# A decoder layer with RWKV-7 and forgetting attention: the order of the substitution's loads and copies, and the number format of two per-head sums

## The chip, the cores and the metric

The kernel runs on one core of a Trainium2 chip. The metric is device time in microseconds of one execution, here the median of three runs. Engines are called as in the profile: PE (TensorE, matmul), PEld (its weight loads), DVE (VectorE), ACT (ScalarE), POOL (GpSimd), SP (SyncE, which issues all the DMAs of this kernel).

## The reference

One layer over 1024 tokens of width 1024, in float32: a norm, one projection to 14 blocks of 128 columns for RWKV-7 and to those of a forgetting attention (8 heads of 64 for each of the two), the two groups of heads, an output projection, and a gated MLP with a causal convolution. What the change touches lies in the RWKV part:

```python
kk = heads(k * k_k)
kk = kk * lax.rsqrt(jnp.maximum(jnp.sum(kk * kk, axis=-1, keepdims=True), 1e-24))
k = k * (1.0 + (a - 1.0) * k_a)
y = wkv7_scan(r_h, w_h, k_h, v_h, -kk, kk * a_h)
...
bonus = jnp.sum(r_h * k_h * r_k, axis=-1, keepdims=True) * v_h
```

`wkv7_scan` is a recurrence over tokens, `S = S * w + (S a) b + v k`, one 64 x 64 state for each head.

## The kernel before, in words

**Stages.** First comes the RWKV stage: 8 units, a unit being two heads (a pair `p`, 128 channels on the partitions) and one half (`hf`) of the tokens, with the dense projections (`r_...` and `t_...` matmuls, groups 0 to 14) beside it. When all 8 units have their output, the attention starts (`s` scores, `t` transposes of the softmax, `po` value products, `tt` transposes of the output), with what is left of the dense work beside it; its last two head pairs ask for all dense groups. The output projection (`op`) may begin once the dense work is done. Then comes the MLP, which takes the rest of the span.

**A unit.** The recurrence is worked in chunks of 64 tokens. `front` loads keys and rates, sums squares over a head's channels (`ss`), and makes decayed operands. `gram` multiplies them to 64 x 64 matrices, whose masked triangles go to `ga` and `gr`. `taken_out` sends the 32 x 32 diagonal blocks of `ga` to DRAM (`dsub`). `inverse` brings them back as 128 partitions with a block's columns on each (`ml`, of 32 rows; `mw`, 8 of them, the block columns that a partition solves), and inverts the triangles by substitution: 30 steps of one multiplication and one addition on POOL, four memsets of the diagonal, and stores to DRAM (`dinv`). `placed` loads these as block-diagonal weights (`tbd`). `solve` starts with parts that don't need them (`z`), then multiplies by `tbd`, by the off-diagonal blocks and by `tbd` again (`x`, `l`, `xx`). `chain` runs the state through 8 chunks, and `output` norms and gates. `slots` turns keys and values and makes the second sum over a head's channels, `bps`, from `rk` = r k r_k. Both sums are a matmul with `oblk`, a 128 x 128 matrix with ones in its two 64 x 64 diagonal blocks: each column of the result is the sum over the column's head, on all its partitions.

**What sets the order.** Each step is a generator that yields instructions. A planner with a cost for each instruction picks at each moment the one that can start first on its engine, and among those that could start at once, the one with the lowest number in `RANK`; the dense work has 9, `inverse` 7, `placed` 6, `taken_out` 0. The result is one fixed order for each engine, and each engine works it off in that order, waiting where an operand is not there. Each of the nine steps of a unit is one stream (`each`) that takes the units one after the other. `ml`, `mw` and `ga` have one buffer each.

**Formats.** A float32 matmul runs as several passes. The dense projections instead split each operand into a part rounded to a shorter format (float32r, `hi`, a cast on ACT) and the rest (`lo`, a subtraction on DVE), and multiply those in one pass each. `Q.take(fp, ..., "f2", ..., 4)` takes one of four places of a ring in SBUF, when the place is free again; the evacuations of the dense matmuls draw from the same ring.

Of the kernel before, what the change touches and what calls it, by code (L numbers as in the profile page):

```python
# [8 lines left out]
F32 = mybir.dt.float32  # L9
F32R = mybir.dt.float32r  # L10
AF = mybir.ActivationFunctionType
ALU = mybir.AluOpType
# [4 lines left out]
P = 128  # L17
# [3 lines left out]
HALF = 512  # L21
# [11 lines left out]
INF = float("inf")  # L33

RANK = dict(rates=4, loads=2, params=4, fills=3, normed=4, turned=4, weights=3, splits=3, dense=9, evac=0, forget=8,
            chain=1, solve=2, inverse=7, taken_out=0, placed=6, front=3, gram=0, slots=4, output=5, stages=0, late_splits=8,
            late_loads=3, late=9, products=5, load_pairs=6, values=3, scores=0, soft=4, turned_back=2, tail=7,
            added=3, parts=1, summed=4, turned_again=4, combined=2, up_loads=6, sums=2.5, up_splits=2.5, down_loads=7,
            down_splits=2.5, token_loads=5, conv=9, combined_2=3,
# [235 lines left out]
def hymba_layer(tc, x, norm_mix_w, w_in, rwkv_mu, rwkv_w0, rwkv_w2, rwkv_a0, rwkv_a2, rwkv_g2, rwkv_k_k, rwkv_k_a,  # L275
# [3 lines left out]
    PE, V, S, G, SP = (Queue(k, e) for k, e in (("PE", nc.tensor), ("V", nc.vector), ("S", nc.scalar),  # L279
                                                ("G", nc.gpsimd), ("SP", nc.sync)))  # L280
    Q = Streams()

    whole = ExitStack()
    with whole:
        whole.enter_context(tc.manual_schedule())
        cst = whole.enter_context(tc.tile_pool(name="cst", bufs=1))
# [3 lines left out]
        ident = cst.tile([P, P], F32, name="ident")  # L290
        make_identity(nc, ident)
        Q.given.update([ident.name] + [f"in_{n}" for n in _INS])
        oblk = cst.tile([P, P], F32, name="oblk")
        ones = cst.tile([P, P], F32, name="ones")
        mhalf = cst.tile([P, 16], F32, name="mhalf")
        prm = cst.tile([P, C_END], F32, name="prm")
        cvw = cst.tile([P, 3, 2 * NFF], F32, name="cvw")
        Q.do(V.memset(mhalf, -0.5), V.memset(oblk, 0.0), V.memset(oblk[0:64, 0:64], 1.0),
             V.memset(oblk[64:128, 64:128], 1.0), V.memset(ones, 1.0),)


        sp_r = {(j, p, h): dr.tile([P, HALF], F32, name=f"sp_{j}_{p}_{h}") for j in "rkv" for p in range(4)
# [28 lines left out]
        fp = whole.enter_context(tc.tile_pool(name="fp", bufs=2))  # L331
# [8 lines left out]
        def bank(tag, name, bufs):  # L340
            t = yield from Q.take(pd if tag == "mm" else pr_, [P, HALF], F32, tag, name, bufs)
            return t
# [398 lines left out]
        def has(i, key):  # L741
            return lambda: i < 0 or key in units[i]

        def names(i):
# [11 lines left out]

            return p, hf, u, tl, rp, col

        def front(i):
            p, hf, u, tl, rp, col = names(i)  # L760
            q = units[i]
            yield lambda: ("rate", p, hf) in done and ("r", 4 + p, hf) in done
            xs = tl("t2", "xs", [P, HALF], 6)
            yield SP.dma_start(xs, sp_th[0, p, hf])
            kt_ = tl("ld", "k", [P, HALF], 2)
            yield SP.dma_start(kt_, sp_r["k", p, hf])
            ta = tl("t2", "ta", [P, HALF], 6)
            yield SP.dma_start(ta, sp_th[1, p, hf])
            k3 = kt_.rearrange("p (n c) -> p n c", c=C)


            sq = tl("t2", "sq", [P, HALF], 6)
            yield S.activation(sq, kt_, AF.Square, scale=col(C_KK))
            pt = yield from rp("ss")
            yield PE.matmul(pt, lhsT=oblk, rhs=sq, start=True, stop=True)
            beta = tl("t2", "beta", [P, HALF], 6)
            yield V.tensor_scalar(beta, pt, scalar1=1e-24, scalar2=0.0, op0=ALU.max, op1=ALU.add)
            Q.release(pt)

            cum = tl("cx", "cum", [P, 8, C + 1], 2)  # L780
            yield V.memset(cum[:, :, 0:1], 0.0)
            for n in range(8):
                yield V.tensor_tensor_scan(cum[:, n, 1:C + 1], xs[:, n * C:(n + 1) * C], ones[:, 0:C], 0.0,
                                           op0=ALU.add, op1=ALU.add)
            cr = tl("cx", "cr", [P, 8, C + 1], 2)
            yield V.tensor_tensor(cr, cum, cum[:, :, 32:33].to_broadcast([P, 8, C + 1]), op=ALU.subtract)
            ex = tl("cx", "ex", [P, 8, C + 1], 2)
            yield S.activation(ex, cr, AF.Exp, scale=-SDEC)


            em = tl("t2", "em", [P, HALF], 6)
            yield S.activation(em.rearrange("p (n c) -> p n c", c=C), cr[:, :, 1:C + 1], AF.Exp, scale=SDEC)
            ke = tl("t2", "ke", [P, HALF], 6)
            yield S.activation(ke, ta, AF.Identity, scale=hka[:, p:p + 1], bias=oka[:, p:p + 1])
            for n in range(4):
                yield V.reciprocal(beta[:, n * P:(n + 1) * P], beta[:, n * P:(n + 1) * P])
            yield lambda: ("r", p, hf) in done
            yield has(i - 1, "bonus")
            rt = tl("ld", "r", [P, HALF], 2)
            yield SP.dma_start(rt, sp_r["r", p, hf])  # L800
            r3 = rt.rearrange("p (n c) -> p n c", c=C)
            fx = Q.tile(sm, [P, 9], F32, "fx", f"{u}_fx", 2)
            yield V.tensor_tensor(fx[:, 0:7], cr[:, 0:7, C], cr[:, 1:8, 0], op=ALU.subtract)
            yield V.tensor_copy(fx[:, 7:8], cr[:, 7, C:C + 1])
            yield V.tensor_scalar(fx[:, 8:9], cr[:, 0, 0:1], scalar1=-1.0, scalar2=0.0, op0=ALU.mult, op1=ALU.add)
            yield has(i - 3, "chain")
            ff = Q.tile(sm, [P, 9], F32, "ff", f"{u}_ff", 3)
            yield S.activation(ff, fx, AF.Exp, scale=-SDEC)
            yield V.tensor_scalar(ta, ta, scalar1=0.5, scalar2=0.5, op0=ALU.mult, op1=ALU.add)
            yield V.scalar_tensor_tensor(ta, kt_, col(C_KK), ta, op0=ALU.mult, op1=ALU.mult)  # L810
            yield has(i - 1, "kbt")
            kb = tl("kb", "kb", [P, 4, 4, C], 1)
            ta4 = ta.rearrange("p (m o c) -> p m o c", o=2, c=C)
            em4 = em.rearrange("p (m o c) -> p m o c", o=2, c=C)
            ke4 = ke.rearrange("p (m o c) -> p m o c", o=2, c=C)
            yield V.tensor_tensor(kb[:, :, 0::3, :], ta4, em4, op=ALU.mult)
            yield V.tensor_tensor(ke, ke, kt_, op=ALU.mult)
            yield V.tensor_tensor(kb[:, :, 1:3, :], ke4, em4, op=ALU.mult)
            yield has(i - 1, "taken")
            ar = tl("ar", "ar", [P, 2, 8, C], 1)  # L820
            yield V.scalar_tensor_tensor(ar[:, 0], k3, nkk[:, p:p + 1], ex[:, :, 0:C], op0=ALU.mult, op1=ALU.mult)
            yield V.tensor_tensor(ar[:, 0], ar[:, 0], beta.rearrange("p (n c) -> p n c", c=C), op=ALU.mult)
            yield V.tensor_tensor(ar[:, 1], r3, ex[:, :, 1:C + 1], op=ALU.mult)
            yield V.scalar_tensor_tensor(rt, rt, col(C_RK), ke, op0=ALU.mult, op1=ALU.mult)
            q.update(kb=kb, ar=ar, ff=ff, rk=rt, front=True)
# [32 lines left out]
        def slots(i):  # L858

            p, hf, u, tl, rp, col = names(i)  # L860
            q = units[i]
# [24 lines left out]
            yield S.copy(vu4[0:64, :, 1, :], pt[64:128].rearrange("p (m c) -> p m c", c=P))  # L886
            Q.release(pt)
            q["vu"] = vu
            pt = yield from rp("bps")
            yield PE.matmul(pt, lhsT=oblk, rhs=q["rk"], start=True, stop=True)  # L890
            q["bonus"] = True
            yield V.tensor_tensor(bv, bv, pt, op=ALU.mult)
            Q.release(pt)
# [15 lines left out]
        def inverse(i):  # L909


            p, hf, u, tl, rp, col = names(i)
            q = units[i]
            yield has(i, "dsub")
            dsub = q["dsub"]
            dinv = dr.tile([8, 2, 2, 32, 32], F32, name=f"{u}_dinv")
            ml = tl("ml", "ml", [P, 32, 32], 1)
            mw = tl("mw", "mw", [P, 8, 32], 1)
            tmp = tl("mtmp", "mtmp", [P, 72], 1)
            mwf = mw.rearrange("p a t -> p (a t)")  # L920
            for g in range(4):
                gs = slice(g * 32, g * 32 + 32)
                yield SP.dma_start(ml[gs], dsub.rearrange("q o b s t -> (q o b) s t"))
                yield S.copy(mw[gs], ml[gs, g::4, :])
            for s in range(1, 31):
                w, n = 31 - s, (s + 3) // 4
                tv = tmp[:, 0:n * w].rearrange("p (s t) -> p s t", t=w)
                yield G.tensor_tensor(tv, mw[:, 0:n, s:s + 1].to_broadcast([P, n, w]),
                                      ml[:, s:s + 1, s + 1:32].to_broadcast([P, n, w]), op=ALU.mult)
                yield G.tensor_tensor(mw[:, 0:n, s + 1:32], mw[:, 0:n, s + 1:32], tv, op=ALU.add)  # L930
            for g in range(4):
                yield G.memset(mwf[g * 32:g * 32 + 32, g::36], 1.0)
            for g in range(4):
                yield SP.dma_start(dinv.rearrange("q o b s t -> (q o b) s t")[:, g::4, :],
                                   mw[g * 32:g * 32 + 32])
            q["dinv"] = dinv

        def placed(i):
            q = units[i]
# [1047 lines left out]
```

## Time and profile before

| | |
|---|---|
| three runs, us | 1462.61, 1462.68, 1465.28 |
| profiled execution, us | 1458.29 |
| its span, first to last instruction, us | 1456.5 |
| granted PE clock, mean | 0.996 |
| first score matmul of the attention, us from the span's start | 552.42 |

In slices of 1/40 of the span (36.4 us; digits are busy tenths) POOL shows where the substitution runs, and PE that it is full nearly everywhere but in the first slice, about the sixteenth to twentieth, and in the last:

```profile
PE   6999999999999999989999989999999999999997
POOL 3006553365465212433301000000000000000011
```

The costs on POOL: 240 multiplications (30 for each unit) and as many additions (columns: busy us and mean ns of one, then idle time before them and what ended it).

```profile
L193 POOL TENSOR_TENSOR u_mtmp<-u_mw,u_ml 128x60 f32<-128x60 f32 (+10 forms) x240 | 79.1, 330 | 147.7 <-ACT u_mw L193 129.6
L193 POOL TENSOR_TENSOR u_mw<-u_mw,u_mtmp 128x60 f32<-128x60 f32 (+10 forms) x240 | 83.9, 350 | 18.6
```

All instructions are recorded by one helper, so all have line 193; groups are told apart by their tiles. In the profile a unit's tiles are called `u_...`, whatever the unit.

### The profile page before, as it was taken

How to read it: one execution, taken by the hardware profiler on the slowest of the kernel's cores; microseconds unless marked ns; L12 is line 12 of the kernel's file. 1: busy time of each engine (PE TensorE's matmuls, PEld its weight loads, DVE VectorE, ACT ScalarE, POOL GpSimd, SP SyncE). 2: the span in 40 equal slices, each digit the busy share in tenths (PEclk: the TensorE clock that was granted, in tenths of full speed). 3: DMA queues.
4: the chain of work that ended last, by engine and by line, in shares of the span. 5: the costliest groups of instructions: out<-in, count | busy, mean ns of one | idle time of the engine just before them, and what ended most of it. 6: DMA issues, size and time to landing. Idle time of an engine off the chain costs nothing.

```text
span 1456.5 us, 23416 instructions
## 1 busy us (share of the span) xinstructions
PE 1404.3 (96%) x8105; PEld 1159.0 (80%) x8105; DVE 1061.2 (73%) x2036; ACT 712.8 (49%) x1339; POOL 300.6 (21%) x772
## 2 busy tenths in 40 slices
PE   6999999999999999989999989999999999999997
PEld 4777877889999998667678868888888888888886
DVE  5387567877775546787546898988887776896575
ACT  6643344445343336777533654455544544444453
POOL 3006553365465212433301000000000000000011
PEclk9999999999999999999999999999999999999999
DMA  5544333433422335474271134555652225864342
GB/s 178 195 120 136 97 95 111 123 102 100 113 68 78 87 104 154 136 213 132 90 267 65 62 113 156 190 188 195 202 167 80 73 86 187 305 199 139 95 152 87
DMA packets 198099, 198.12 MB, mean 136 GB/s; under 512 B 39979, under 2 KB 135773, under 8 KB 197981
## 3 DMA queue, kind: packets, MB, share of 16 engines
q1 hardware_dynamic: 197981, 196.63, 43.5%
q8 instruction: 64, 1.05, 0.3%
q14 instruction: 54, 0.44, 0.1%
HBM read 139.13 MB, written 57.44 MB: 135 GB/s over the span
## 4 chain that ended last, share of the span: by engine, by line
PE 77%; DVE 9%; DMA 6%; issue 3%; ACT 3%; SPq 1%; POOL 1%; DVEq 0%; POOLq 0%; ACTq 0%
PE B L193 16%; PE t L193 9%; PE r L193 8%; PE C L193 8%; PE dx L193 8%; PE dy L193 6%; PE op L193 4%; PE A L193 4%; PE u_uy L193 1%; DMA qraw<-sp_q 1%; PE s L193 1%; SPq L193 1%; PE po L193 1%; DMA x<-in_x 1%; DMA raw<-in_w_out 1%
## 5 line engine op out<-in xcount | busy, mean ns | idle before, releaser
L193 PE MATMUL t<-whi,hhi 128*128 128x256 f32 (+1 forms) x512 | 149.5, 292 | 1.2 <-ACT whi L193 0.8
L193 PE MATMUL t<-whi,hlo 128*128 128x256 f32 (+1 forms) x512 | 149.8, 293 | 0.0
L193 PE MATMUL t<-wlo,hhi 128*128 128x256 f32 (+1 forms) x512 | 149.1, 291 | 0.3 <-DVE wlo L193 0.3
L193 POOL TENSOR_SCALAR fms<-fms 128x1 f32<-128x1 f32 x8 | 2.4, 295 | 609.4 <-ACT fsq L193 609.1
L193 POOL TENSOR_TENSOR u_mtmp<-u_mw,u_ml 128x60 f32<-128x60 f32 (+10 forms) x240 | 79.1, 330 | 147.7 <-ACT u_mw L193 129.6
L193 ACT CAST dwhiP<-dP 128x512 fp32r<-128x512 f32 x77 | 47.7, 620 | 107.6 <-PE dy L193 48.4
L193 PEld LDWEIGHTS t<-whi,hhi 128*128 128x128 f32 x512 | 96.6, 189 | 3.6 <-ACT whi L193 1.0
L193 PEld LDWEIGHTS t<-wlo,hhi 128*128 128x128 f32 x512 | 96.6, 189 | 2.0 <-issue 1.0
L193 PEld LDWEIGHTS t<-whi,hlo 128*128 128x128 f32 x512 | 96.7, 189 | 1.9 <-issue 1.4
L193 PE MATMUL r<-hhi,whi 128*128 128x512 f32 x224 | 92.1, 411 | 0.9 <-DVE edge L193 0.6
L193 PE MATMUL r<-hlo,whi 128*128 128x512 f32 x224 | 92.7, 414 | 0.0
L193 PE MATMUL r<-hhi,wlo 128*128 128x512 f32 x224 | 91.7, 410 | 0.5 <-DVE wlo L193 0.5
L193 DVE TENSOR_TENSOR dwloP<-dP,dwhiP 128x512 fp32r<-128x512 f32 x77 | 53.1, 689 | 51.2 <-ACT dwhiP L193 50.8
L193 POOL TENSOR_TENSOR u_mw<-u_mw,u_mtmp 128x60 f32<-128x60 f32 (+10 forms) x240 | 83.9, 350 | 18.6
L193 DVE SCALAR_TENSOR_TENSOR yv<-uv,cvw,yv 128x1023 f32<-128x1023 f32 (+1 forms) x44 | 56.3, 1280 | 38.9 <-ACT yv L193 38.8
L193 PE MATMUL dx<-dwhiP,glP 128*128 128x512 f32 x176 | 69.4, 394 | 0.0
L193 PE MATMUL dx<-dwhiP,ghP 128*128 128x512 f32 x176 | 69.4, 394 | 0.0
L193 PE MATMUL dx<-dwloP,ghP 128*128 128x512 f32 x176 | 69.0, 392 | 0.0
L193 DVE SCALAR_TENSOR_TENSOR yg<-ug,cvw,yg 128x1023 f32<-128x1023 f32 (+1 forms) x44 | 56.4, 1282 | 7.6 <-ACT yg L193 6.7
L193 ACT CAST whi<-wraw 128x512 fp32r<-128x512 f32 (+1 forms) x60 | 37.0, 619 | 38.8 <-PE r L193 17.6
L193 ACT ACTIVATE pr<-pr,mx 128x1024 f32<-128x1024 f32 (+7 forms) x64 | 49.6, 779 | 9.3 <-DVE mx L193 9.1
L193 DVE TENSOR_TENSOR glP<-gb,ghP 128x512 fp32r<-128x512 f32 x77 | 52.7, 684 | 0.7 <-ACT ghP L193 0.6
(953 smaller groups left out, 4123.4 us busy)
## 6 DMA issues: line engine op xcount, KB each, us to landing
a<-in_ffn_w_up SPq DMA_DIRECT2D x88, 256.0 KB
wraw<-in_w_in SPq DMA_DIRECT2D x108, 128.0 KB
sp_gv<-yg SPq DMA_DIRECT2D x22, 512.0 KB
dB<-in_ffn_w_down SPq DMA_DIRECT2D x44, 256.0 KB
sp_T<-dB SPq DMA_DIRECT2D x44, 256.0 KB
gb<-sp_gv SPq DMA_DIRECT2D x44, 256.0 KB
dP<-sp_T SPq DMA_DIRECT2D x44, 256.0 KB
dP<-in_ffn_w_down SPq DMA_DIRECT2D x33, 256.0 KB
```

The source lines that it names most:

```text
L193: fn(*args, **kw)
```

## The change

Two things are done.

The first: the four loads of `ml` are all issued before the four copies to `mw`, which had alternated with them. Loads, copies and the stores of `dinv` now have rank 0 in place of 7; the 30 steps and the memsets become a stream of their own, `substituted`, which keeps rank 7, and `inverse` waits for it before it stores. `placed` goes from rank 6 to 0.

The second: a helper `head_sums` replaces the f32 matmul with `oblk` in both sums. It rounds the operand (`hi`, on ACT), subtracts (`lo`, on DVE), takes two places of the ring `f2` for them, and multiplies both by `oblk`, which is now made in the rounded format.

```diff
-            chain=1, solve=2, inverse=7, taken_out=0, placed=6, front=3, gram=0, slots=4, output=5, stages=0, late_splits=8,
+            chain=1, solve=2, inverse=0, taken_out=0, substituted=7, placed=0, front=3, gram=0, slots=4, output=5, stages=0, late_splits=8,
...
-        oblk = cst.tile([P, P], F32, name="oblk")
+        oblk = cst.tile([P, P], F32R, name="oblk")
...
+        def head_sums(name, src):
+            hi = yield from Q.take(fp, [P, HALF], F32R, "f2", f"{name}_hi", 4)
+            yield S.copy(hi, src)
+            lo = yield from Q.take(fp, [P, HALF], F32R, "f2", f"{name}_lo", 4)
+            yield V.tensor_tensor(lo, src, hi, op=ALU.subtract)
+            pt = yield from bank("rp", name, 3)
+            yield [PE.matmul(pt, lhsT=oblk, rhs=hi, start=True, stop=False),
+                   PE.matmul(pt, lhsT=oblk, rhs=lo, start=False, stop=True)]
+            Q.release(hi)
+            Q.release(lo)
+            return pt
...
-            pt = yield from rp("ss")
-            yield PE.matmul(pt, lhsT=oblk, rhs=sq, start=True, stop=True)
+            pt = yield from head_sums(f"{u}_ss", sq)
...
-            pt = yield from rp("bps")
-            yield PE.matmul(pt, lhsT=oblk, rhs=q["rk"], start=True, stop=True)
+            pt = yield from head_sums(f"{u}_bps", q["rk"])
...
+            quarters = [slice(g * 32, g * 32 + 32) for g in range(4)]
+            for gs in quarters:
+                yield SP.dma_start(ml[gs], dsub.rearrange("q o b s t -> (q o b) s t"))
+            for g, gs in enumerate(quarters):
+                yield S.copy(mw[gs], ml[gs, g::4, :])
+            Q.spawn("substituted", substituted(q, ml, mw, tmp))
+            yield has(i, "substituted")
+            for g in range(4):
+                yield SP.dma_start(dinv.rearrange("q o b s t -> (q o b) s t")[:, g::4, :],
+                                   mw[g * 32:g * 32 + 32])
+            q["dinv"] = dinv
+        def substituted(q, ml, mw, tmp):
             mwf = mw.rearrange("p a t -> p (a t)")
-            for g in range(4):
-                gs = slice(g * 32, g * 32 + 32)
-                yield SP.dma_start(ml[gs], dsub.rearrange("q o b s t -> (q o b) s t"))
-                yield S.copy(mw[gs], ml[gs, g::4, :])
             for s in range(1, 31):
...
+            q["substituted"] = True
```

The planner makes a new order from this, over the whole RWKV stage and the attention. Three places of it follow.

SP, where unit u20 (pair 2, first half) brings its blocks back. Before (`sp_v`, `sp_g` are stores of the attention's values and gates, `sg` a load of `output`):

```order
L193 DMA u20_dsub_3206<-u20_ga_3131 32x8x32 x4
L193 DMA u10_sg_3230<-sp_sg_0_117 128x512
L193 DMA tbd_271<-u11_dinv_2666 32x8x32 x4
L193 DMA u20_ml_3236<-u20_dsub_3206 32x1024
L193 DMA sp_v_3_138<-vt_3_2_3275 128x128
L193 DMA sp_g_3_142<-vt_3_2_3275 128x128
L193 DMA u20_ml_3236<-u20_dsub_3206 32x1024
L193 DMA sp_v_3_138<-vt_3_3_3323 128x128
L193 DMA sp_g_3_142<-vt_3_3_3323 128x128
L193 DMA u20_ml_3236<-u20_dsub_3206 32x1024 x2
```

The same place after the change:

```order
L193 DMA wraw_8_0_3186<-in_w_in 128x2x128 x2
L193 DMA u20_dsub_3221<-u20_ga_3132 32x8x32 x4
L193 DMA wraw_8_1_3227<-in_w_in 128x2x128 x2
L193 DMA u20_ml_3247<-u20_dsub_3221 32x1024 x4
L193 DMA sp_v_3_138<-vt_3_0_3357 128x128
```

The loads stand together now, and the `tbd` of the unit before has been loaded earlier.

PE, where the same unit sums its squares. Before (`r_6_0_0` is a dense matmul of group 6, `kbt` transposes of another unit):

```order
L193 MATMUL r_6_0_0_2511<-hhi_251,whi_6_3_2514 128x512
L193 MATMUL u20_ss_2622<-u20_sq_2593,oblk_67 128x512
L193 MATMUL u11_kbt0_2643<-ident_62,u11_kb_2427 128x128 x4
L193 MATMUL r_6_0_0_2511<-hhi_251,wlo_6_3_2515 128x512
L193 MATMUL u11_kbt1_2654<-ident_62,u11_kb_2427 128x128 x4
```

After:

```order
L193 MATMUL u10_l1_2661<-u10_x1_2452,l32_272 128x128 x4
L193 MATMUL u20_ss_2658<-u20_ss_hi_2604,oblk_67 128x512
L193 MATMUL u20_ss_2658<-u20_ss_lo_2610,oblk_67 128x512
L193 MATMUL r_5_1_1_2548<-hhi_251,whi_5_2_2178 128x512
L193 MATMUL r_5_1_1_2548<-hhi_251,wlo_5_2_2179 128x512
```

The sum is two matmuls, and it stands a dense group earlier: beside group 5 instead of group 6.

PE in the attention, second head pair (`s22`, `s23` are scores of the blocks 22 and 23, `t210` and the like transposes of their softmax). Before:

```order
L193 MATMUL s23_0_7683<-k11_7193,qhi111_7400 128x512
L193 MATMUL s23_0_7683<-k11_7193,qlo111_7401 128x512
L193 MATMUL s23_512_7741<-k11_7193,qhi111_7400 128x128
L193 MATMUL s23_512_7741<-k11_7193,qlo111_7401 128x128
L193 MATMUL t210_7709<-ident_62,pr21_7635 128x128 x4
L193 MATMUL t214_7757<-ident_62,pr21_7635 128x128 x2
```

After (`t_14_6` is a dense matmul of the last group):

```order
L193 MATMUL s22_0_7693<-k10_7170,qhi110_7183 128x512
L193 MATMUL s22_0_7693<-k10_7170,qlo110_7184 128x512
L193 MATMUL s22_512_7708<-k10_7170,qhi110_7183 128x128
L193 MATMUL s22_512_7708<-k10_7170,qlo110_7184 128x128
L193 MATMUL t_14_6_7520<-whi_14_3_6840,hlo_252 128x256
L193 MATMUL t_14_6_7520<-whi_14_3_6840,hhi_251 128x256
L193 MATMUL t200_7706<-ident_62,pr20_7641 128x128 x4
```

Dense matmuls stand here; in the old order the last of them stood between the blocks 16 and 20. Counted over the whole order, 226 dense matmuls (of 1536 with 256 or 264 columns) stand behind the first score matmul, where 115 did; 40 matmuls of `op` stand ahead of the last value product, where 63 did. Between the last Gram matmul and the first solve matmul of the last unit, u31, 261 dense matmuls stand instead of 359.

More of the change, by code (lines that the diff above doesn't have):

```diff
@@ L297, in hymba_layer @@
         cvw = cst.tile([P, 3, 2 * NFF], F32, name="cvw")
-        Q.do(V.memset(mhalf, -0.5), V.memset(oblk, 0.0), V.memset(oblk[0:64, 0:64], 1.0),
-             V.memset(oblk[64:128, 64:128], 1.0), V.memset(ones, 1.0),)
+        Q.do(V.memset(mhalf, -0.5), V.memset(ones, 1.0),
+             V.tensor_scalar(oblk, ones, scalar1=0.0, scalar2=0.0, op0=ALU.mult, op1=ALU.add),
+             V.tensor_copy(oblk[0:64, 0:64], ones[0:64, 0:64]), V.tensor_copy(oblk[64:128, 64:128], ones[64:128, 64:128]))
         sp_r = {(j, p, h): dr.tile([P, HALF], F32, name=f"sp_{j}_{p}_{h}") for j in "rkv" for p in range(4)
@@ L932, in inverse @@
                 yield G.memset(mwf[g * 32:g * 32 + 32, g::36], 1.0)
[L933 to L936, printed above, removed]
+            q["substituted"] = True
         def placed(i):
```

## The prediction

> **What bounds the kernel now.** I read the page's first lines and its chain first, since they say which engine the end hangs on.
>
> ```profile
> span 1456.5 us, 23416 instructions
> PE 1404.3 (96%) x8105; PEld 1159.0 (80%) x8105; DVE 1061.2 (73%) x2036; ACT 712.8 (49%) x1339; POOL 300.6 (21%) x772
> PE 77%; DVE 9%; DMA 6%; issue 3%; ACT 3%; SPq 1%; POOL 1%; DVEq 0%; POOLq 0%; ACTq 0%
> ```
>
> TensorE is busy for 96% and holds 77% of the chain. So the question for every edit is whether it takes work from PE, or fills one of PE's gaps. The windows view says where the gaps are (columns: stretch, length, then busy us of PE, PEld, DVE, ACT, POOL, clock, DMA share, GB/s).
>
> ```profile
> 60.00:540.00 480.00, 471.92 (x3590) 409.55 (x3589) 329.31 (x813) 197.82 (x398) 203.56 (x553) 1.00 0.38 106
> 540.00:720.00 180.00, 166.09 (x1162) 129.34 (x1161) 127.91 (x350) 123.38 (x298) 63.97 (x135) 0.99 0.49 144
> 720.00:800.00 80.00, 76.02 (x340) 59.79 (x339) 43.41 (x66) 28.21 (x58) 7.92 (x21) 1.00 0.49 165
> 880.00:1456.00 576.00, 568.78 (x2476) 464.56 (x2474) 452.31 (x633) 274.27 (x441) 10.51 (x24) 1.00 0.48 158
> ```
>
> The first row is the RWKV stage, with the dense projections as filler: PE idles 480.00 - 471.92 = 8.1 us in it. The second is the attention: 13.9 us idle in 180. The long last one has 7.2 us, all after the last matmul. A second call cuts the attention up.
>
> ```profile
> 580.00:640.00 60.00, 52.52 (x364) 38.24 (x362) 44.87 (x123) 46.66 (x118) 22.41 (x45) 0.97 0.52 155
> 640.00:720.00 80.00, 76.42 (x515) 57.68 (x515) 58.33 (x171) 54.60 (x139) 31.61 (x73) 1.00 0.44 129
> ```
>
> 60.00 - 52.52 = 7.5 of the 13.9 us lie in 580 to 640: by the order of instructions the dense matmuls have run out there and the first output projections (`op`) have not begun, so nothing fills PE's waits for the softmax. These are its longest, from 540 to 780 (total us, times, longest):
>
> ```profile
> PE s L193 <- DVE mx L193: 3.1, 5, 1.2
> PE op L193 <- ACT cwhi L193: 3.0, 3, 2.4
> ```
>
> **Part 1: the sums over a head's channels.** 16 of them (two in each of 8 units) go from one f32 matmul to two in the rounded format.
>
> ```profile
> 308.36 1.02 PE L193 MATMUL u_bps<-u_r,oblk 128*128 128x512 f32 x2
> 309.31 0.45 PE L193 MATMUL u_uy<-u_vu,u_gr 128*64 128x64 f32 x8
> 745.21 22.57 PE op L193 x98
> ```
>
> An f32 sum holds PE from 308.36 until the next matmul starts at 309.31: 0.95 us (the trace shows it as two instructions). For the rounded format the measure is the row of `op`, a piece of the chain of waits, with other weights at every matmul: 22.57 / 98 = 0.23 us each, so two take 0.46. That saves 0.49 us, and 16 x 0.49 = 7.8 us. [...] I take **-7**, with 7.8 as the upper end and, as the lower, the 1.8 that the last rival works out.
>
> What it adds lies on other engines: a cast on ACT, a subtraction on DVE for each sum.
>
> ```profile
> L193 ACT CAST whi<-wraw 128x512 fp32r<-128x512 f32 x46 | 28.5, 619 | 30.6 <-PE r L193 12.0 <-PE t L193 9.4 <-DMA wraw<-in_w_in 8.9
> L193 DVE TENSOR_TENSOR wlo<-wraw,whi 128x512 fp32r<-128x512 f32 (+1 forms) x50 | 34.6, 696 | 8.2 <-ACT whi L193 7.7
> ```
>
> 16 x 0.62 = 9.9 us on ACT (197.82 of 480 busy) and 16 x 0.70 = 11.1 on DVE (329.31 of 480): both have room in the RWKV stage, and PE has dense work meanwhile. It costs something where the pair stands in PE's fixed order and its `lo` is late: PE then stops with all that is behind it. The same stop exists today for `ss`, behind ScalarE's square:
>
> ```profile
> PE u_ss L193 <- ACT u_sq L193: 0.7, 2, 0.4
> ```
>
> 0.35 us a time, in 2 of the 5 units between 80 and 320. If all 16 sums stopped so, now behind two more instructions, that would be 5.6 us; if none, 0. The two halves also take two of the four places of the ring `f2`, from which the projections' evacuations draw; they are held for about a cast, a subtraction and a matmul, some 2 us, against a unit's 45.
>
> **Part 2: the substitution.** Before, load and copy alternate, and other transfers of SP come between. Two units show both patterns (first u11, whose four loads happened to be issued together; then u20).
>
> ```profile
> 236.52 1.76 SPq L193 DMA_DIRECT2D u_ml<-u_dsub  x4
> 241.62 0.24 POOL L193 TENSOR_TENSOR u_mtmp<-u_mw,u_ml 128x30 f32<-128x30 f32 x1 [20.05 <-ACT u_mw L193]
> ...
> 281.93 0.38 SPq L193 DMA_DIRECT2D u_ml<-u_dsub  x1
> 285.09 1.17 SPq L193 DMA_DIRECT2D u_ml<-u_dsub  x1
> 287.26 0.89 SPq L193 DMA_DIRECT2D u_ml<-u_dsub  x2
> 291.52 0.23 POOL L193 TENSOR_TENSOR u_mtmp<-u_mw,u_ml 128x30 f32<-128x30 f32 x1
> ```
>
> Together: 241.62 - 236.52 = 5.1 us from the first load to the first step on POOL. Apart: 9.6. In the last unit, u31, it is 16.8:
>
> ```profile
> 432.23 0.42 SPq L193 DMA_DIRECT2D u_ml<-u_dsub  x1
> 449.07 0.24 POOL L193 TENSOR_TENSOR u_mtmp<-u_mw,u_ml 128x30 f32<-128x30 f32 x1 [8.02 <-ACT u_mw L193]
> ```
>
> After the change all eight units have the first pattern, and the higher ranks bring the stores of `dinv` and the loads of `tbd` forward in SP's order. That is 4 to 12 us a unit off a path from which chain and output hang. None of it is PE's time: the stage is full of dense matmuls. What it does is to **end the RWKV stage earlier, so that more dense work is left for the attention**. How much, the new order says: behind the first score matmul stand 226 dense matmuls, before 115; and ahead of the last value product stand 40 `op`, before 63.
>
> ```profile
> 525.43 8.37 PE t L193 x69
> ```
>
> A dense matmul takes 8.37 / 69 = 0.121 us: 111 x 0.121 = 13.4 us of filler move in, and 23 x 0.23 = 5.3 us of `op` move out behind the attention: 8.1 us net. What is worth money is the part that lands in idle time. New dense rows stand beside the second head pair, where the 7.5 us were; 6.4 us lie elsewhere. Bounds: 0 (the waits come back at other places) and 8.1. I take half, **-4**.
>
> **Part 3: new waits.** The order expects the inverses earlier, too. Between u31's last Gram matmul and its first solve matmul stand 261 dense matmuls instead of 359, 98 x 0.121 = 11.9 us less cover; the path saves 16.8 - 5.1 = 11.7 on the loads and what it gains on SP's queue. So the room stays about as tight as it was, and it hangs on POOL's steps.
>
> ```profile
> 268.44 0.58 POOL L193 MEMSET u_mw<- 32x8 f32 x4
> ...
> 395.00 0.24 POOL L193 TENSOR_TENSOR u_mtmp<-u_mw,u_ml 128x30 f32<-128x30 f32 x1 [4.11 <-ACT u_mw L193]
> 427.32 0.58 POOL L193 MEMSET u_mw<- 32x8 f32 x4
> ```
>
> u11 took 269.0 - 241.6 = 27.4 us, u30 427.9 - 395.0 = 32.9. Why the spread, the timeline tells:
>
> ```profile
> 416.12 0.30 POOL L193 TENSOR_TENSOR u_mtmp<-u_mw,u_ml 128x60 f32<-128x60 f32 x1
> 416.49 1.53 POOL L193 TENSOR_TENSOR u_mw<-u_mw,u_mtmp 128x60 f32<-128x60 f32 x1
> 416.52 0.67 DVE L193 TENSOR_TENSOR u_kb<-u_ke,u_em 128x512 f32<-128x512 f32 x1
> 417.12 0.74 DVE L193 SCALAR_TENSOR_TENSOR u_ar<-u_k,nkk,u_ex 128x512 f32<-128x512 f32 x1
> ```
>
> A step whose neighbour takes 0.30 took 1.53 while DVE ran two operations on pairs of SBUF tiles. The new subtraction (`src`, `hi`) is one more of this kind, so it slows the very steps that the change wants sooner. [...]
>
> From rows alone, 0.70 us is the most that one subtraction can add on POOL, 2 x 0.70 = 1.4 us a unit, about what the room takes up. I charge **+2** for all new waits. Lower bound -2 (the stops at `ss` may also go), upper +12 (5.6 at the sums, and u30's excess of 32.9 - 27.4 = 5.5 once in full, rounded up).
>
> **The sum.** -7 - 4 + 2 = -9 us, against the profiled execution's 1458.29 us (span 1456.5 and 1.8 around it). The median, 1462.68, is 4.4 above that execution; 1462.68 - 9 = **1453.7 us**.
>
> **Rivals.**
> - *All the shifted filler lands.* Dense rows stand just where PE idled; against it, PE's waits in the attention are for DVE and ACT, which run on their own pace. -7.8 - 8.1 and no new wait: 1446.8.
> - *Given back.* The stops at the sums and at the solve take all that was won: -7 - 0 + 7 (5.6 at the sums, 1.4 at a solve), 1462.7. For it: the chain is short of slack in every unit. Against: no solve matmul is among PE's long waits today.
> - *Slower: POOL is late and SP stands.* SP issues in order. The stores of `dinv`, moved forward, wait on SP for POOL's last step, with weight loads and all the other loads behind them, and PE stops at the solve. It decides from about 30 us on POOL a unit, between u11's 27.4, which made no stop, and u30's 32.9: then each unit costs its excess, at 32.9 some 3 us, 8 x 3 = 24. 24 - 7 - 4 = +13: 1475.7. For it: u30; against: u11's 27.4 and the copies of ACT that no longer alternate with loads.
> - *Not what it says.* If loading the weights of the block matrix twice showed, a pair would cost 0.46 + 2 x 0.19 (PEld, 189 ns in the page's rows) = 0.84, and the sums would save 0.11 x 16 = 1.8 in place of 7. The row of `op` speaks against it: it loads weights each time and steps at 0.23. 1462.68 - 1.8 - 4 + 2 = 1458.9.
>
> ```profile
> L193 PEld LDWEIGHTS t<-whi,hhi 128*128 128x128 f32 x512 | 96.6, 189 | 3.6 <-ACT whi L193 1.0
> ```
>
> **How the numbers follow.** Forecast (-4 to -14) 0.55, all filler 0.12, not what it says 0.05, given back 0.14, slower 0.14. A change of this kernel's time can be told from none from about 0.2%, 2.9 us, on. The forecast, the full filler and, with its -3.8, the fourth rival are faster: 0.72; given back is the same for nearly all of its chance: 0.13; slower 0.15. The range takes in the lower bounds (-7.8 - 8.1 - 2 = -17.9: 1444.8, rounded to 1445) and reaches to +2 (1464.7, rounded to 1464), which leaves out most of the slower case and little else.
>
> **What would show it right or wrong.** A pair of sum matmuls should hold PE for 0.46 us (wrong: near 0.95). First load to first POOL step about 5 us in each unit. The first score matmul,
>
> ```profile
> 552.42 0.47 PE L193 MATMUL s<-k,qhi 128*128 128x512 f32 x1 [0.52 <-POOL qr_r L193]
> ```
>
> should stand near 533 (552.4 - 13.4 for the dense work moved behind it, - 7 for the sums, + 1); PE's idle time in the attention some 4 us less and none of it in a stretch without filler. No PE wait on `tbd` among the longest. The forecast is wrong if the RWKV stage doesn't end some 15 us earlier, if POOL's steps grow beyond 30 us a unit, or if the attention lengthens by as much as it starts sooner.

## The result, and the profile after

The changed kernel takes 1453.65 us (median of five runs, 1450.91 to 1458.52), the one before 1462.68 (1462.21 to 1465.28). The ratio is 0.9942, 95% interval 0.9924 to 0.996: faster, by 9.0 us or 0.6%, as forecast to a tenth. A second set of five runs gave 1454.57 against 1461.32, ratio 0.9955 (0.9941 to 0.9969). The profiled execution took 1453.65 us, against 1458.29. The page's first lines and the chain:

```profile
span 1452.0 us, 23487 instructions
PE 1401.8 (97%) x8105; PEld 1165.2 (80%) x8105; DVE 1071.0 (74%) x2051; ACT 719.9 (50%) x1356; POOL 297.8 (21%) x772
PE 65%; DVE 4%; DMA 3%; issue 2%; ACT 2%; POOL 1%; SPq 0%; DVEq 0%; POOLq 0%; ACTq 0%
```

PE leads still (the shares add up to 77%: the chain could not be followed to the start). The changed sums, where a unit makes `bps` (columns: start, duration, engine, tiles; matmuls overlap, so the pitch of the starts counts):

```profile
303.18 0.50 PE L193 MATMUL u_bps<-u_bps_hi,oblk 128*128 128x512 f32 x1
303.52 0.39 PE L193 MATMUL u_bps<-u_bps_lo,oblk 128*128 128x512 f32 x1
303.75 0.29 PE L193 MATMUL t<-whi,hlo 128*128 128x264 f32 x1
```

The second pass takes 303.75 - 303.52 = 0.23 us, the first, behind an f32 matmul, 0.34. The pair takes 0.57 here, and 0.46 in the units where rounded matmuls stand ahead of it. Now the substitution, in u31:

```profile
425.35 3.43 SPq L193 DMA_DIRECT2D u_ml<-u_dsub  x4
431.96 0.24 POOL L193 TENSOR_TENSOR u_mtmp<-u_mw,u_ml 128x30 f32<-128x30 f32 x1
459.23 0.58 POOL L193 MEMSET u_mw<- 32x8 f32 x4
468.89 3.29 SPq L193 DMA_DIRECT2D tbd<-u_dinv  x4
534.99 0.47 PE L193 MATMUL s<-k,qhi 128*128 128x512 f32 x1 [1.00 <-issue]
```

First load to first step: 6.6 us in place of 16.8; over the eight units 4.7 to 6.9, mean 5.9 for 10.6. The first score matmul starts at 534.99, 17.4 us sooner. By the windows view, cut where each kernel's first score and last value product stand (stretch, length, then busy us of PE, PEld, DVE, ACT, POOL, clock, DMA share, GB/s), first the kernel before:

```profile
60.00:552.00 492.00, 482.69 (x3675) 419.72 (x3673) 333.43 (x820) 202.05 (x406) 205.07 (x555) 1.00 0.39 109
552.00:713.50 161.50, 149.60 (x1046) 114.79 (x1048) 120.94 (x335) 117.60 (x286) 59.19 (x127) 0.99 0.48 140
```

and the changed one:

```profile
60.00:535.00 475.00, 466.36 (x3570) 409.45 (x3568) 339.57 (x830) 206.36 (x417) 200.84 (x554) 1.00 0.40 110
535.00:703.00 168.00, 156.63 (x1134) 124.71 (x1136) 122.02 (x338) 120.21 (x292) 60.31 (x126) 0.99 0.49 140
```

The RWKV stage is 17 us shorter and the attention 6.5 us longer: the filler moved, as the order said. But PE's idle time in the attention is 168.00 - 156.63 = 11.4 us, where it was 161.50 - 149.60 = 11.9 before: it hardly fell. Where it went, three stretches of the changed kernel tell:

```profile
580.00:640.00 60.00, 51.92 (x359) 39.37 (x357) 42.96 (x121) 43.19 (x107) 23.21 (x49) 0.97 0.57 168
535.00:615.00 80.00, 75.84 (x581) 65.43 (x582) 54.02 (x144) 53.39 (x122) 23.03 (x52) 1.00 0.45 130
615.00:640.00 25.00, 20.86 (x131) 14.18 (x129) 20.11 (x54) 19.26 (x50) 11.22 (x21) 0.93 0.74 221
```

In 580 to 640, where the prediction counted 7.5 us of idle time, there are now 60.00 - 51.92 = 8.1. The last dense matmul ends at 615.4 (at 596.9 before). As long as dense work stands beside the attention, PE idles 4.2 of 80 us, and in the 25 us behind it 4.1. Before, by the same view, it was 2.2 of 45 (552 to 597) and 6.9 of 43 (597 to 640). So the idle share is about a twentieth with filler and a sixth without, in both kernels: the stretch without filler got shorter, and the one with filler got longer by more.

PE's long waits are the old ones (540 to 780; total us, times, longest):

```profile
PE s L193 <- DVE mx L193: 3.1, 5, 1.1
PE op L193 <- ACT cwhi L193: 2.7, 2, 2.4
```

The solve does not stop: PE's waits for `tbd` are 0.6 and 0.9 us in all between 80 and 320 and between 320 and 540. So the total came out as forecast, and one of its terms did not. The runs below take the terms apart.

### The profile page after: what moved, and what is told of

Same layout as the page of the kernel before. It is cut to its first block, busy times and chain, and to the rows that moved or that the text cites. A ratio compares the mean times of both kernels' runs of the same rounds, so it can differ in the third digit from the quotient of the medians.

```text
span 1452.0 us, 23487 instructions
## 1 busy us (share of the span) xinstructions
PE 1401.8 (97%) x8105; PEld 1165.2 (80%) x8105; DVE 1071.0 (74%) x2051; ACT 719.9 (50%) x1356; POOL 297.8 (21%) x772
## 4 chain that ended last, share of the span: by engine, by line
PE 65%; DVE 4%; DMA 3%; issue 2%; ACT 2%; POOL 1%; SPq 0%; DVEq 0%; POOLq 0%; ACTq 0%
PE B L193 16%; PE t L193 9%; PE C L193 8%; PE dx L193 8%; PE dy L193 6%; PE op L193 6%; PE A L193 4%; PE s L193 2%; DMA qraw<-sp_q 1%; PE po L193 1%; PE u_uy L193 1%; PE D L193 1%; DVE pr L193 1%; SPq L193 0%; PE hT L193 0%
## 5 line engine op out<-in xcount | busy, mean ns | idle before, releaser
L193 DVE TENSOR_TENSOR wlo<-wraw,whi 128x512 fp32r<-128x512 f32 (+1 forms) x60 | 41.5, 694 | 19.2 <-ACT whi L193 18.8
```

The source lines that it names most:

```text
L193: fn(*args, **kw)
```

## The experiments

All times are medians, ratios are against the kernel before on the same chip.

**One half of the change alone.** e1 has the new sums with the old substitution and ranks (and one more place in the ring of the row sums `rsum`, which leaves the order of the kernel before as it is):

```diff
-            chain=1, solve=2, inverse=0, taken_out=0, substituted=7, placed=0, front=3, gram=0, slots=4, output=5, stages=0, late_splits=8,
+            chain=1, solve=2, inverse=7, taken_out=0, placed=6, front=3, gram=0, slots=4, output=5, stages=0, late_splits=8,
...
-            for gs in quarters:
+            for g in range(4):
+                gs = slice(g * 32, g * 32 + 32)
                 yield SP.dma_start(ml[gs], dsub.rearrange("q o b s t -> (q o b) s t"))
-            for g, gs in enumerate(quarters):
                 yield S.copy(mw[gs], ml[gs, g::4, :])
```

> Only the sums are changed; the substitution is as before (one ring of small tiles has six places instead of five, which the new order needs). By the new order no dense matmul stands behind the first score matmul (before 115) and 96 matmuls of the output projection ahead of the last value product (before 63): 13.9 us of dense filler leave the attention and 7.6 us of op come in, net 6.3 out. Theory of the forecast (sums 7 us, half of the shifted filler counts): -7 + 3 = -4, near 1459, with more PE idle time in the attention than before. Rival (only the matmuls count, the reordering is worth nothing): -7, near 1456, with PE's idle time as before. Rival (the sums save little, the substitution did it): within 2 us of before.

1495.56 us, ratio 1.023 (1.021 to 1.0251): 34 us slower than the kernel before, which has 1461.7 beside it. Neither the theory nor a rival had expected a loss. e2 is the other half, the kernel before with the new `inverse`, `substituted` and ranks:

```diff
-            chain=1, solve=2, inverse=7, taken_out=0, placed=6, front=3, gram=0, slots=4, output=5, stages=0, late_splits=8,
+            chain=1, solve=2, inverse=0, taken_out=0, substituted=7, placed=0, front=3, gram=0, slots=4, output=5, stages=0, late_splits=8,
...
-            for g in range(4):
-                gs = slice(g * 32, g * 32 + 32)
+            for gs in quarters:
                 yield SP.dma_start(ml[gs], dsub.rearrange("q o b s t -> (q o b) s t"))
+            for g, gs in enumerate(quarters):
                 yield S.copy(mw[gs], ml[gs, g::4, :])
+            Q.spawn("substituted", substituted(q, ml, mw, tmp))
```

> Only the substitution is changed (loads together, own stream, new ranks); the sums are f32 matmuls. By the new order 299 dense matmuls stand behind the first score matmul (before 115) and 35 of op ahead of the last value product (before 63): +22.3 and -6.4, net 15.9 us of filler into the attention. Theory of the forecast: half of it, -8, with little for new waits: near 1455. Rival (only the matmuls count): 1462 to 1463. In both, POOL's first step comes some 5 us after the first load in every unit.

1464.85 us, ratio 1.0023 (1.0008 to 1.0038), so not the 1455 of the forecast's theory. The halves are +34 and +3 alone and -9 together: they don't add. The trace of e2 shows what became of the filler when the substitution stands alone; its attention in the windows view:

```profile
531.00:710.00 179.00, 166.72 (x1208) 134.33 (x1208) 123.12 (x339) 122.57 (x295) 60.90 (x127) 0.98 0.45 134
```

Its first score starts at 531.6, 20.8 us sooner than before, with 299 dense matmuls behind it in place of 115. The attention is 179.00 - 161.50 = 17.5 us longer, and PE still idles 179.00 - 166.72 = 12.3 us in it. The filler that came in lengthened the stage and left the idle time as it was.

The loss of e1 is of another kind. Its u31, and PE where the attention should begin:

```profile
452.21 0.32 SPq L193 DMA_DIRECT2D u_ml<-u_dsub  x1
458.78 0.46 SPq L193 DMA_DIRECT2D u_ml<-u_dsub  x1
463.71 0.46 SPq L193 DMA_DIRECT2D u_ml<-u_dsub  x1
465.70 0.43 SPq L193 DMA_DIRECT2D u_ml<-u_dsub  x1
469.72 0.24 POOL L193 TENSOR_TENSOR u_mtmp<-u_mw,u_ml 128x30 f32<-128x30 f32 x1 [14.52 <-ACT u_mw L193]
...
486.03 0.20 POOL L193 TENSOR_SCALAR qr_a<-qms 128x8 f32<-128x8 f32 x1 [2.25 <-DVE qms L193]
486.31 1.65 POOL L193 TENSOR_TENSOR qr_r<-qr_a,mhalf 128x8 f32<-128x8 f32 x1
...
515.35 0.97 SPq L193 DMA_DIRECT2D tbd<-u_dinv  x2
...
577.02 0.80 PE L193 MATMUL op<-cwhi,hhi 128*128 128x512 f32 x1 [8.40 <-ACT hhi L193]
...
583.49 0.76 PE L193 MATMUL s<-k,qhi 128*128 128x512 f32 x1 [1.94 <-issue]
```

The loads alternate with copies for 17.5 us; the steps take 39.3 us on POOL (22.1 before), since the attention's query norms (`qr`, four here) stand among them in POOL's order and two of them wait for DVE; the last `tbd` load stands at 515.9 where it stood at 486.6 before. The planner had meanwhile put all dense work ahead of the first score (0 dense matmuls behind it). The last runs at 561.6, and from its end to the first score, 21.6 us, PE finds 5.4 us of work: the end of the last unit, transposes, and six matmuls of `op`. In slices of 5 us:

```profile
560.00:565.00 5.00, 3.29 (x23) 2.43 (x21) 2.67 (x5) 2.66 (x6) 2.81 (x4) 1.00 0.16 54
565.00:570.00 5.00, 0.76 (x5) 0.42 (x4) 3.44 (x7) 1.68 (x4) 1.47 (x1) 0.86 0.29 107
570.00:575.00 5.00, 0.00 (x0) 0.00 (x0) 1.04 (x3) 1.23 (x2) 0.00 (x0) 0.50 0.73 238
580.00:585.00 5.00, 3.06 (x6) 1.71 (x7) 1.87 (x3) 1.76 (x4) 0.29 (x1) 0.50 0.98 273
585.00:590.00 5.00, 4.27 (x14) 2.85 (x14) 4.67 (x10) 3.41 (x6) 0.00 (x0) 0.50 0.48 145
```

PE idles, and the clock (third number from the end) is at half for 23.9 us, from 568.6 on. The attention has no filler at all:

```profile
583.50:757.50 174.00, 150.84 (x938) 108.39 (x940) 112.52 (x318) 108.53 (x265) 50.49 (x115) 0.94 0.39 114
```

23.2 us idle, twice what it was. Over the whole span PE idles 75.3 us, 23.1 more than in the profile before, and is busy for 1418.5 instead of 1404.3, although the sums take some 5 us less. The clock is at half for 60.3 us in all, where it was for 12.8. What it is in the sums that makes the planner stretch the units so was not isolated.

**Which part of the substitution's edit undoes this.** Both runs have the new sums. e3 keeps the grouped loads and takes the old ranks; e4 keeps the ranks and lets loads and copies alternate.

```diff
-            chain=1, solve=2, inverse=0, taken_out=0, substituted=7, placed=0, front=3, gram=0, slots=4, output=5, stages=0, late_splits=8,
+            chain=1, solve=2, inverse=7, taken_out=0, substituted=7, placed=6, front=3, gram=0, slots=4, output=5, stages=0, late_splits=8,
```

> The changed kernel with the ranks of before (inverse 7, placed 6): loads together and the stream of its own stay, the sums too. By the order 106 dense matmuls stand behind the first score matmul and 78 of op ahead of the last value product: the RWKV stage hardly ends earlier than before. Theory of the forecast: -7 for the sums, -1 for 2.4 us of filler: near 1455; if the ranks carry the gain of the substitution, it is slower than the changed kernel by 2 to 4 us, and if the grouping of the loads does, it is the same.

```diff
-            for gs in quarters:
-                yield SP.dma_start(ml[gs], dsub.rearrange("q o b s t -> (q o b) s t"))
             for g, gs in enumerate(quarters):
+                yield SP.dma_start(ml[gs], dsub.rearrange("q o b s t -> (q o b) s t"))
                 yield S.copy(mw[gs], ml[gs, g::4, :])
```

> The changed kernel with loads and copies alternating as before; the new ranks, the stream and the sums stay. By the order 29 dense matmuls stand behind the first score matmul and 96 of op ahead of the last value product: net 2.8 us less filler in the attention than before. Theory of the forecast: -7 + 1.4 = -5.6, near 1457, 3 us slower than the changed kernel; the first POOL step comes 8 to 10 us after the first load. Rival (only the matmuls count): as the changed kernel.

e3 1457.77 us, 0.9979 (0.9965 to 0.9992); e4 1464.34, 1.0019 (1.0004 to 1.0034). With the new sums: neither 1495.6, ranks 1464.3, grouping 1457.8, both 1453.7. Each run undoes most of the 34 us. Both also have the steps as a stream of their own, which e1 has not, and no run has that stream alone, so its share is not shown. Once one of the two is there, the grouping is worth some 10 us and the ranks 4; e4 came out slower than either of its expectations. The runs further down show that an order alone moves the time by 4 to 9 us, so the 4 are not told from a new order. In all of them the first score follows the last load of `tbd` by 60 to 68 us (486.6 to 552.4 before, 471.7 to 535.0 after, 491.0 to 553.4 in e3, 500.8 to 560.8 in e4, 515.8 to 583.5 in e1). This fits that the edits act by when u31's inverse is there; no run moved that alone.

**The terms in one and the same order.** These keep the changed kernel's order, instruction for instruction. The planner plans with the changed kernel's instructions, and `Q.instead` puts another in the place of one of them, or nothing (`None`), when the program is written out. A second run of the changed kernel stands beside them.

> The changed kernel once more, on the chip of the three that follow, so that these are compared with it side by side. Both theories: 9 us below the kernel before, 1453 to 1455 where that has 1462 to 1463.

e7 leaves the `lo` matmul out:

```diff
-            yield [PE.matmul(pt, lhsT=oblk, rhs=hi, start=True, stop=False),
-                   PE.matmul(pt, lhsT=oblk, rhs=lo, start=False, stop=True)]
+            planned = [PE.matmul(pt, lhsT=oblk, rhs=hi, start=True, stop=True),
+                       PE.matmul(pt, lhsT=oblk, rhs=lo, start=False, stop=True)]
+            Q.instead[id(planned[1])] = None
+            yield planned
```

> The changed kernel in the very same order, with the second matmul of each sum (the one over the rest) left out: the sums are then those of the rounded operands alone. Nothing else moves. It takes 16 x 0.23 = 3.7 us from PE and nothing else. If a microsecond of PE in the RWKV stage is a microsecond of the end: 3.7 us below the changed kernel, near 1450. If the other engines set the pace there: as the changed kernel.

e8 keeps casts and subtractions, and makes the sum by the old f32 matmul on the operand itself (`oblk` in f32):

```diff
+            Q.instead[id(planned[0])] = PE.matmul(pt, lhsT=oblk, rhs=src, start=True, stop=True)
+            Q.instead[id(planned[1])] = None
```

> The changed kernel in the very same order, but where the two rounded matmuls of a sum stood, the one f32 matmul of before; the casts and subtractions are still done, and not used. It measures the first term of the forecast alone: 6.4 to 7.8 us above the changed kernel, near 1460 to 1461. Rival (PE waits there for others anyway): less than 3 us above.

e9 is e8 without the casts and subtractions:

```diff
+            cast = S.copy(hi, src)
+            Q.instead[id(cast)] = None
...
+            rest = V.tensor_tensor(lo, src, hi, op=ALU.subtract)
+            Q.instead[id(rest)] = None
```

> The changed kernel's order with the sums of before altogether: the f32 matmul, and no casts and no subtractions. Against the one before it in this list it measures what the added work on ACT and DVE costs (forecast: 2 us, so 1458 to 1459; rival, that work is hidden: the same time). Against the kernel before it measures the new order alone: by the forecast -4 (1458.7); by the finding that the substitution alone brought nothing, 1462 to 1465.

| kernel | us | ratio (95%) |
|---|---|---|
| changed kernel again | 1454.57 | 0.9955 (0.9941 to 0.9969) |
| e7, one pass | 1449.88 | 0.9927 (0.9915 to 0.9939) |
| e8, f32 sums | 1458.95 | 0.9982 (0.997 to 0.9995) |
| e9, f32 sums, no casts | 1459.24 | 0.9991 (0.9979 to 1.0002) |

The format is worth 1458.95 - 1454.57 = 4.4 us (by the two intervals, give or take some 2.7), a single pass 4.7 (expected from 16 x 0.23: 3.7). The 4.4 lie between what the theory (6.4 to 7.8) and the rival (less than 3) expected. What the casts and subtractions cost, e8 against e9, is -0.3, give or take some 2.4: none that can be told, though the forecast's 2 us are not far outside. And the new order with the old sums, e9 against before, brings 2.1, which its interval doesn't tell from nothing. That the format's gain is made in the RWKV stage, the first score matmul shows, in the second run of the changed kernel

```profile
532.72 0.47 PE L193 MATMUL s<-k,qhi 128*128 128x512 f32 x1 [0.35 <-issue]
```

and in e8:

```profile
539.29 0.47 PE L199 MATMUL s<-k,qhi 128*128 128x512 f32 x1
```

6.6 us apart, in the same order. One execution's mark is good to 2 or 3 us only: the first execution of the changed kernel has it at 534.99, 4.3 ahead of e8, and e7, with 3.7 us less work on PE, at 532.65, no sooner than the second. By the starts of the matmuls, an f32 sum holds PE for 0.86 us behind a rounded matmul that it follows without a wait (in the kernel before at 103.1, 405.3 and 453.5) and 0.96 behind an f32 one of 64 columns (259.6); the pair takes 0.46 and 0.57. The difference is 0.40 or 0.39, and 16 x 0.40 = 6.4 us; by the starts of all 16 it is 5.7 between these two executions, since some pairs take longer.

**How much of a time belongs to one order.** A latency that the planner uses, ("V","SP"), goes from 0.2 to 0.21 us. Nothing that is computed changes; the order does, a little.

```diff
-           ("V", "G"): 0.1, ("V", "SP"): 0.2, ("S", "PE"): 0.3, ("S", "V"): 0.15, ("S", "G"): 0.15, ("S", "SP"): 0.0,
+           ("V", "G"): 0.1, ("V", "SP"): 0.21, ("S", "PE"): 0.3, ("S", "V"): 0.15, ("S", "G"): 0.15, ("S", "SP"): 0.0,
```

> The sums alone once more (the substitution as before), with one latency of the planner, from DVE to SP, at 0.21 instead of 0.20 us, which makes it draw another order of the same work. By that order, too, no dense matmul stands behind the first score matmul and 96 of op ahead of the last value product. If the loss of the sums alone comes from dense work that runs out before the RWKV stage ends: again 1485 to 1500. If it was an accident of one order: 1455 to 1465.

> The kernel before with the same small change of that latency: the same work in another order (to the first score matmul the same, behind it 91 instead of 63 matmuls of op ahead of the last value product). It measures how far the time moves by a new order alone. If orders with the same dense work behind the first score matmul are alike: within 2 us of before.

> The changed kernel with the same small change of that latency; 208 dense matmuls behind the first score matmul instead of 226, 36 of op ahead of the last value product instead of 40. If the gain belongs to the change and not to one lucky order: 1452 to 1457, 6 to 9 us below before. If to the order: 1457 to 1465.

The kernel before comes to 1458.23, 0.9979 (0.9966 to 0.9992), the changed kernel to 1462.63, 1.0012 (0.9998 to 1.0026), the sums alone to 1492.82, 1.0224 (1.0204 to 1.0243). So an order moves the time by -3.6 (2 had been expected at most) and by +8 to +9 us for no reason in the work. With this latency the changed kernel falls where its expectation said that the gain would belong to the order, and it is 4.4 us slower than the kernel before with the same latency, instead of 9 faster. The 31 us of the sums alone stay. What the kernel before gained is not seen in its waits: PE idles 51.9 us over the span, as before (52.2). The changed kernel idles 57.9 for 50.2. What it lost, PE's waits from 540 to 780 and the first score tell:

```profile
PE s L193 <- ACT qhi L193: 6.2, 4, 2.4
PE s L193 <- DVE mx L193: 4.5, 7, 1.2
...
539.38 0.77 PE L193 MATMUL s<-k,qhi 128*128 128x512 f32 x1 [2.89 <-POOL nb L193]
```

PE waits 2.89 us for one small POOL result before the first score, 6.2 in four waits for `qhi`; the 2.89 us are followed by 3.4 us of half clock:

```profile
539.20:542.60 3.40, 3.22 (x11) 2.86 (x12) 1.99 (x4) 1.22 (x3) 0.00 (x0) 0.50 0.77 200
```

## Why the prediction was right, and where it wasn't

**The bound** was read rightly: PE is full (in its row of 40 slices only the 18th and the 24th are below nine tenths, beside the first and the last), and in the changed kernel's profile the 16 sums take 5.3 us less of it by the starts of all of them (at 0.39 each it would be 6.3), and PE idles 50.2 us over the whole span in place of 52.2. Together that is most of the 9.0 us between the medians. The two profiled executions differ by less, 4.6 us, and PE's busy time on their pages by 2.5, since the clock was lower in the second: at 0.993 of 1452.0 us, 10.2 us are lost, and at 0.996 of 1456.5 only 5.8. The kernel before had 0.992 to 0.993 as the median clock of its later runs, so its profiled execution had an uncommonly high one. To add the terms to the median, and not to that execution, was right.

**Part 1** (-7): the mechanism stands, and the size, the author's estimate below the 7.8 of the rows, is right within its bounds: 5.3 by the matmuls' starts, 4.3 or 6.6 at the first score, 4.4 (some 2 to 7) at the end. What no row could show, the loss behind a matmul of the other format, is 0.11 us a pair behind an f32 matmul of 64 columns (0.57 for 0.46), but the f32 sum pays 0.10 there too (0.96 for 0.86), so it cancels. Behind an f32 matmul of 128 columns it does not: the pair takes 0.54 to 0.58 (168.7, 227.4 and 275.9), an f32 sum 0.86 (before, 210.4). The fourth rival, "Loading the weights twice shows", is out: the second pass steps at 0.23.

**Part 2** (-4) has the step that failed: "What is worth money is the part that lands in idle time", of which I took half. The loads did what was forecast (5.9 us in the mean), the stage ended 17.4 us sooner, 8 us of filler moved in. But the dense matmuls did not land in idle time: 11.9 us of it before, 11.4 after, and 12.3 in e2 with still more filler. PE still waits for a twentieth of the time with dense work beside the attention, and there is now more of that time. What e9 measures for the order is -2.1 (-0.21% to +0.02%, so -3.1 to +0.3 us), and e2's own new order cost 3. The prediction's third way to be wrong, "the attention lengthens by as much as it starts sooner", came true for the filler: of the 17.4 us, the attention takes back 7.0 (161.1 to 168.1, first score to last value product) and the output projection, whose `op` moved behind it, 4.5 (86.1 to 90.6); 5.9 are left at the start of the MLP, about the PE work that the sums save.

**Part 3** (+2) was near nothing, as far as it was measured: -0.3, give or take 2.4, for the casts and subtractions in the fixed order. Two of the 16 pairs (at 73.8 and 109.8) stop PE for a late `lo` and take 0.76 and 0.85 us in place of 0.46. POOL does stop beside the new subtractions; `u_bps_lo` ran from 299.96 to 300.65 here:

```profile
299.67 0.26 POOL L193 TENSOR_TENSOR u_mw<-u_mw,u_mtmp 128x35 f32<-128x35 f32 x1
300.01 0.74 POOL L193 TENSOR_TENSOR u_mtmp<-u_mw,u_ml 128x28 f32<-128x28 f32 x1
300.83 0.24 POOL L193 TENSOR_TENSOR u_mw<-u_mw,u_mtmp 128x28 f32<-128x28 f32 x1
```

A step of 0.24 takes 0.74. Seven steps began while such a subtraction ran; they are 0.33 to 0.51 us longer than steps of their form beside no DVE operation, 0.38 in the mean, half of the 0.70 that I had as a bound. Each is longer by what was left of the subtraction, less 0.14 us. A unit takes 27.3 us on POOL as the mean (26.9 before). Two take 34.9 and 31.1, which the prediction had named as a sign of being wrong, and PE hardly waits for `tbd`: the 30 us at which I let the slower rival begin is too low. A late inverse can cost much, though: in e1, where the last unit's takes 17.5 + 39.3 us, the kernel loses 34 us. There it is not SP's order that stands, but dense work that has run out.

**What the forecast lacked altogether** is that the two halves depend on each other. I priced the sums as if they could stand in the old order; alone they are 34 us slower, and with a new latency 31, and it is the substitution's edit that makes them affordable. And the forecast's ±10 us had no term for the order itself, which is worth -4 to +9. That the median fell within 0.1 us of the forecast is chance: -4 and +2 were each about 2 off, in opposite directions, and with another latency of the planner the gain is gone. The terms by e8 and e9 (-4.4, -0.3 and -2.1) add up to the -6.8 of the second set because they are the steps between its runs, so the sum confirms nothing. The first set's -9.0 has an interval of -11 to -6.

## What to carry to other kernels

Where a planner makes the order, price an edit in a fixed order first (replace the operations and keep the rest), and vary a number that should not matter to see how far the order alone moves the time: here the format was worth some 4 to 6 us and the order up to 9. Test the parts of a change alone and together; one of them may pay only because the other shortened a path that it would have lengthened. Filler moved to a stage is worth what idle time it takes away there, and where it takes away none, as here in the attention, the stage gets longer by it.

## What the runs showed of the hardware

PE's clock falls to half for 3.41 us or multiples of it, in the middle of a kernel that keeps PE 97% busy: in the changed kernel's profile for 3.41 us at 622.47 and at 721.45 and for 6.83 at 837.51, in e1's for 23.9, seven times 3.41. These stretches start whole multiples of 3.41 us apart (29 and 34 times 3.41 in the changed kernel). To see when, I divided the 13 profiled executions, from 45 us to shortly before the end, into slices on the grid of these stretches and took PE's busy share of each slice that was at full clock. Of 23 slices with a share below 0.4, all were followed by half clock; of 21 from 0.4 to 0.5, 16; of 19 from 0.5 to 0.6, 3; of some 5200 above 0.6, none. So a wait of some 2 us that falls into one slice (of 1.7 to 2 mostly) was mostly followed by half clock. In it an `op` matmul steps at 0.43 us in place of 0.23 (722.8 to 724.5 in the changed kernel), so by an estimate from these numbers such a wait costs up to 3.41 x (1 - 0.23 / 0.43) = 1.6 us more behind it. The longest `op` wait of the kernel before, 2.4 us, is shared by two slices (722.2 to 725.6, of which PE is busy for 0.46, and the next), and no half clock follows (1.00 from 722 to 735). That of the changed kernel, 2.4 us too, falls into one (718.0 to 721.5, share 0.29). It ends at 721.1, and half clock follows from 721.5 to 724.9:

```profile
720.00:725.00 5.00, 3.71 (x9) 2.66 (x9) 2.08 (x3) 1.92 (x4) 0.00 (x0) 0.66 0.90 292
725.00:730.00 5.00, 4.47 (x19) 3.17 (x18) 3.48 (x6) 3.02 (x5) 0.00 (x0) 1.00 0.84 272
```

The stop on POOL has a size: in the nine profiles with the new subtraction, 61 steps of the substitution began while one ran, and each was longer by what was left of it, less 0.13 to 0.15 us. Steps that began before it and met no other DVE operation were not longer (in the changed kernel 0.20, 0.31 and 0.32 us at 204.7, 400.3 and 447.3, within 0.003 of their forms beside no DVE operation).

The first matmul of a pair steps at 0.23 us behind a rounded matmul, the two pairs with a late `lo` aside, and at 0.31 to 0.34 behind an f32 one (all 16 pairs of the changed kernel). An f32 sum, two instructions in the trace, takes 0.43 or 0.53 for the first of them in the kernel before (once 0.50): 0.53 behind an f32 matmul of 64 columns (at 259.6) and behind five waits of 0.11 to 0.44 us (118.6 is one), 0.43 behind rounded matmuls that it follows without a wait and behind f32 ones of 128 columns (210.4 and 375.6). The profile doesn't say why.
